# A hybrid decoder layer in one program: the attention's norm one step later, shorter GpSimd pieces, heads in another order

## The chip, the cores and the metric

The kernel runs on one core of one Trainium2 chip. The metric is the device time of one execution in microseconds (us). Five engines share the work: TensorE (PE; its weight loads are listed apart as PEld), VectorE (DVE), ScalarE (ACT), GpSimd (POOL) and SyncE (SP). SP only issues transfers here, and ACT and POOL issue some of theirs too. Each engine runs its own instructions in program order and waits for others by semaphores.

## The reference

One decoder layer, with `x` of 2048 rows by 1024 columns in float32. A mixer of three head groups is followed by a gated feed-forward network (FFN):

```python
h = _rms(x, norm_mix_g)
z = h @ w_in + b_in                    # 1024 -> 3600 columns, split among the groups
qa, ka = _rms(a_q) , _rms(a_k)         # 8 attention heads of 64 columns
ca = cumsum(log_sigmoid(a_f))          # a forgetting gate per head and row
s  = qa @ ka.T * 64**-0.5 + ca[:, None] - ca[None, :]      # causal
oa = softmax(s) @ a_v
ob = _mlstm_chunkwise(...)             # 4 heads: matrix memory in chunks of 64 rows
oc = _hgrn2_chunkwise(...)             # 4 heads: gated linear attention, chunks of 16
y  = concat(_rms(oa)*g_a, sigmoid(b_o)*_rms(ob)*g_b, silu(c_g)*_rms(oc)*g_c)
x  = x + y @ w_out
x  = x + (silu(conv3(h @ w_up).gate) * conv3(h @ w_up).up) @ w_down   # h = _rms(x), d_ff 2816
```

The attention's output is divided by its softmax sum and then normed over the 64 columns of each head (`_rms(oa)`). The attention heads don't depend on one another, so any order of them gives the same result.

## The kernel before

Matrix products keep float32 accuracy by splitting both operands into a high and a low part (`hi`, `lo`) and adding three products. The high part is a copy in a shorter format on ACT (`AF.Copy`), and the low part is the difference, mostly on POOL. Intermediate results travel through buffers in the chip's memory (`s_qh`, `s_ql`, `s_kh`, `s_kl`, `s_v`, `s_y` and others).

The program has four stages.

1. **The z stage**, up to 924 us. The columns of `z` are projected in groups of 256 (`load_split` loads a group's weights and splits them; L214 is its matmul), for each half of the rows, in the order of the table `ORDER`. Between them run the mLSTM (`phase_b`) and HGRN2 (`phase_c`) blocks, which end in `finish_heads`. Where a q or k group is done, `qk_norm_T` norms it (L418 multiplies by the inverse root on POOL), transposes it and stores it. A v group is copied into a tile per 128 rows (ACT L341, POOL L342) and stored to `s_v` (L345). In this stage each engine's order comes from the framework's scheduler, which places instructions by its own estimates.
2. **The hand-over**, 924 to 950 us, in which the last columns are finished and the first attention head is loaded (`att_load`, SP's queue, L840).
3. **The attention**, 950 to 1396 us, written in a fixed order (`manual_schedule`). A head is 40 steps: four blocks `qb` of 512 rows with 4, 8, 12 and 16 steps `j`. In a step PE computes the scores `s` (L925, L927), ACT the exponential `pf` (L931) and its high part (L933), POOL or on every fourth step DVE the low part `pl` (L937), and PE, three steps later, adds the product with V into `pv` (L950 to L952). The row maxima `mx` of a coming head (PE L874, DVE L878 and L889) run beside it. Work that is due some steps later is put into a list: `later.put(steps, f)` runs `f` that many steps on.
4. **The output projection and the FFN**, from 1396 us to the end; the change doesn't touch them.

Two users of one PSUM tile matter. `k.px` (the name x in the rows) holds in its first 260 columns the four transposes that turn a finished block (`turn`, PE L964, copied away by DVE L967), and behind them three small slots in which the norm of a whole head (`att_finish`, called when the head's last block is done, T steps in) computes its inverse root: `scale` (L1030 to L1032), then `rms_psum` (L981 to L990). `scale` is put 15 steps on. By then the next head has gone on: its block `qb` = 1 ends at the step where its `turn` is due in the same 15th step, and since `scale` was put first, it is issued first.

In the hand-over the last v group (v0) uses tiles named `h` with three buffers, which the transposed q and k (ACT L428) use as well.

Of the kernel before, what the change touches and what calls it, by code (L numbers as in the profile page):

```python
# [49 lines left out]
AHEAD = 4  # L50

ORDER = (
    "ci bv c0 c1 b0 b1 cg bo v1 v0 k0 k1 q0 q1",
    "c0 c1 ci bv b0 b1 cg bo v1 k0 q0 k1 q1 v0",
)
# [122 lines left out]
def load_split(k, wp, src, n=4):  # L178

    nc = k.nc  # L180
    width = src.shape[1]

    k.wn += 1
    at = 64 if k.wn % 2 == 0 and width == 256 else 0
    hi, lo = (
        k.t(wp, [P, 264 * DT], F32R, tag=x)[:, at : at + width * DT].rearrange("p (n c) -> p n c", c=width)
        for x in ("whi", "wlo")
    )
    for q in range(0, DT, n):
        raw = k.t(wp, [P, n, width], tag="wraw")  # L190
        nc.sync.dma_start(raw, src[q * P : (q + n) * P, :].rearrange("(dt p) c -> p dt c", p=P))
        h = hi[:, q : q + n, :]
        nc.scalar.activation(h, raw, AF.Copy)  # L193
        for i in range(0, n, 2):
            nc.gpsimd.tensor_tensor(  # L195
                lo[:, q + i : q + i + 2, :], raw[:, i : i + 2, :], h[:, i : i + 2, :].bitcast(F32), op=ALU.subtract
            )
    return hi, lo
# [64 lines left out]
def z_groups(k, hf, pz, wp, psum, xbufs, rstd=None):  # L263
# [25 lines left out]
    def nat_group(off, kind, g):  # L289
# [4 lines left out]

        store = nc.gpsimd if hf == 1 and off in (OFF_AQ + 256, OFF_AV) else nc.scalar
        bias = k.t(pz, [P, width], tag="bias")
        nc.sync.dma_start(bias, b_in[off : off + width].unsqueeze(0).broadcast_to([P, width]))
        for b in range(2):
# [3 lines left out]
            for tp in range(2):  # L302
# [32 lines left out]
                elif kind[0] == "v":  # L335
                    z4 = z.rearrange("p tt (h d) -> p tt h d", d=HD)
                    for tt in range(2):
                        v = k.t(pz, [P, 4, 130], F32R, tag="h", bufs=3)
                        nc.gpsimd.memset(v[:, :, 64:65].bitcast(F32), 1.0)
                        nc.gpsimd.memset(v[:, :, 129:130].bitcast(F32), 0.0)  # L340
                        nc.scalar.activation(v[:, :, 0:64], z4[:, tt], AF.Copy)  # L341
                        nc.gpsimd.tensor_tensor(  # L342
                            v[:, :, 65:129], z4[:, tt], v[:, :, 0:64].bitcast(F32), op=ALU.subtract
                        )
                        store.dma_start(  # L345
                            k.s_v[t0 + tt * P : t0 + (tt + 1) * P, 4 * g : 4 * g + 4, :], v.bitcast(F32)
                        )
# [60 lines left out]
def qk_norm_T(k, pz, psum, zs, ss, kind, g, store):  # L408
# [6 lines left out]
    for n, (z, hi, t0) in enumerate(zs):  # L415
        z8 = z.rearrange("p tt (h d) -> p (tt h) d", d=HD)
        r8 = rstd[:, 8 * n : 8 * n + 8].unsqueeze(2).broadcast_to([P, 8, HD])
        nc.gpsimd.tensor_tensor(z8, z8, r8, op=ALU.mult)  # L418
        ps = k.t(psum, [P, 2, 2 * P], tag="t", bufs=2)
# [242 lines left out]
def finish_heads(k, pb, num, r, gate, epsf, t0, col, sq, out):  # L662
# [12 lines left out]
    nc.vector.tensor_tensor(out, num, s.unsqueeze(2).broadcast_to([P, 16, HD]), op=ALU.mult)  # L675
    nc.gpsimd.tensor_tensor(out, out, gate.rearrange("p c (h d) -> p (c h) d", d=HD), op=ALU.mult)
    nc.gpsimd.dma_start(
# [5 lines left out]
def phase_c(k, blk, pb, psum):  # L683
# [5 lines left out]
    for j in range(2):  # L689
# [22 lines left out]
        def chunks(x):  # L712
            return x.rearrange("p (c l) -> p c l", l=P)
# [20 lines left out]
        yield  # L734
        for (r, i), eng in zip(heads, engs):
            eng.tensor_tensor(q[r, :, i, :], q[r, :, i, :], chunks(tot[r]), op=ALU.mult)
        h, lv = 1, 0
# [63 lines left out]
    for c in range(0, 4, 2):  # L801
# [4 lines left out]
        nc.vector.scalar_tensor_tensor(gc, gc, 1.0, gz, op0=ALU.add, op1=ALU.mult)  # L806
    nc.gpsimd.tensor_tensor(gate, gate, k.gbc[:, 256:512].unsqueeze(1).broadcast_to([P, 4, 256]), op=ALU.mult)
    num = oc.rearrange("p c j i d -> p (c j i) d")
# [22 lines left out]

def att_load(k, h, st):

    r = slice(h * HD, (h + 1) * HD)
    QA, KA, QB, KB = (k.t(k.pat[f"{t[1]}{h % 2}"], [P, T], F32R, tag=t) for t in ("QA", "KA", "QB", "KB"))
    V = k.t(k.pat[f"V{h % 2}"], [P, 16, 130], F32R, tag="V")
    st.update(QA=QA, KA=KA, QB=QB, KB=KB, V=V, h=h)

    def ld(dst, src):
        k.nc.sync.dma_start(dst.bitcast(F32), src)  # L840

    ld(QB[0:64], k.s_qh[r])
    ld(KB[0:64], k.s_kh[r])
    ld(QB[64:70], k.s_one[0:6])
    ld(KB[64:68], k.s_one[6:10])
    ld(KB[68:70], k.s_fc[h])
    ld(QA[0:64], k.s_qh[r])
    ld(QA[64:128], k.s_ql[r])
    ld(KA[0:64], k.s_kl[r])
    ld(KA[64:128], k.s_kh[r])  # L850
    yield
    v = k.s_v[:, h, :].rearrange("(jt p) c -> p jt c", p=P)
    ld(V[:, 0:4], v[:, 0:4])
    yield
    ld(V[:, 4:16], v[:, 4:16])

# [85 lines left out]
def att_values(k, st, pa, ps, later, qb, j, c0, ph, pl):  # L942

    nc = k.nc
    V, h = st["V"], st["h"]
    if j == 0:
# [14 lines left out]
    def turn(oT):  # L961
# [3 lines left out]
        if qb == 0:  # L965
            st["o"] = k.t(k.pat[f"o{h % 2}"], [P, 16, 65], tag="ao")
        nc.vector.tensor_copy(st["o"][:, 4 * qb : 4 * qb + 4, :], pt)  # L967

    later.put(1, out)
    if h == AH - 1:  # L970
        att_finish(k, st, pa, 4 * qb, 4, later)
    elif qb == 3:
        att_finish(k, st, pa, 0, 16, later)
# [20 lines left out]
def att_finish(k, st, pa, t0, n, later):  # L994
# [7 lines left out]
    pieces = [slice(i, i + 4) for i in range(0, n, 4)]  # L1002
    end = st["h"] == AH - 1 and t0 == 12

# [50 lines left out]
    for c in pieces:  # L1055
        later.put(i, lambda c=c: square(c))
        later.put(i + 1, lambda c=c: total(c))
        i += 1
    i = 15 if n == 16 else i + 1
    later.put(i, scale)  # L1060
# [10 lines left out]
def attention(k, pa, ps, side):  # L1071
# [4 lines left out]
    with k.tc.manual_schedule():  # L1076
        first = att_load(k, 0, sts[0])
        next(first)
        next(first)
# [821 lines left out]
```

## Time and profile before

| | |
|---|---|
| median of 3 runs | 2910.72 us (2910.49 to 2912.88) |
| profiled execution, its own time | 2909.49 us |
| its span in the trace | 2907.7 us |
| mean granted clock of PE | 0.979 |
| busy: PE / DVE / ACT / POOL | 2799.3 / 1961.4 / 1278.8 / 1446.1 us |
| share of the span | 96% / 67% / 44% / 50% |

The span is what the trace covers, from the first to the last instruction, and the execution's own time is 1.8 us longer. PE is the busiest engine by far, so time is lost only where PE waits or where its granted clock is below full speed. The chain that ended last holds only work of the FFN near the program's end; the rows of the earlier stages are therefore read from the waits of PE and from windows.

### The profile page before, as it was taken

To read this page: it belongs to the slowest core of one execution; us is meant where nothing else is said; L and a number is where in the kernel's file an instruction comes from. 1 tells how busy PE (TensorE), PEld (TensorE's weight loads), DVE (VectorE), ACT (ScalarE), POOL (GpSimd) and SP (SyncE) were. 2 spreads that over 40 slices of the span, in tenths; PEclk is the share of its full clock that TensorE was granted. 3 is DMA by queue.
4 is the path that set the end of the run, shared out by engine and by line. 5 is a ranking of instruction groups with operands and counts; after the bars stand their busy time and mean duration, and the time that the engine had idled before them with its cause. 6 is when DMAs were issued, how large, how long until landed. Compare 5 with 4: busy or idle time off the path is not lost. (4 is left out here: it accounts for less than half of the span.)

```text
span 2907.7 us, 42807 instructions
## 1 busy us (share of the span) xinstructions
PE 2799.3 (96%) x15053; PEld 2343.7 (81%) x15053; DVE 1961.4 (67%) x3523; ACT 1278.8 (44%) x2167; POOL 1446.1 (50%) x1255
## 2 busy tenths in 40 slices
PE   7999998999998999999999999999999999999999
PEld 7899996989987766666787788888788788888887
DVE  7336787265777767777446577777787577877655
ACT  4224322131322878887423344444455344344443
POOL 2345462344454668776202566666576444444543
PEclk9999997999998999999999999999999999999999
DMA  5434444333225534450456454445778333333766
GB/s 162 127 95 147 137 128 136 101 96 117 90 90 163 120 89 89 95 120 10 135 171 218 149 166 151 158 159 165 248 252 275 98 100 104 109 106 123 238 206 211
DMA packets 346616, 411.06 MB, mean 141 GB/s; under 512 B 47650, under 2 KB 234096, under 8 KB 343232
## 3 DMA queue, kind: packets, MB, share of 16 engines
q1 hardware_dynamic: 292016, 318.45, 37.0%
q10 hardware_dynamic: 51952, 81.45, 7.7%
q0 software_dynamic: 2432, 8.42, 0.8%
q8 instruction: 118, 1.93, 0.3%
q14 instruction: 98, 0.80, 0.1%
HBM read 280.24 MB, written 127.98 MB: 140 GB/s over the span
## 5 line engine op out<-in xcount | busy, mean ns | idle before, releaser
L1297 POOL TENSOR_TENSOR w<-w,w 128x512 fp32r<-128x512 f32 x302 | 404.3, 1352 | 406.0 <-ACT w L1296 334.8
L1485 PE MATMUL ps<-w,w 128*128 128x512 f32 x1848 | 422.6, 390 | 3.6 <-ACT w L1476 1.9
L1485 PEld LDWEIGHTS ps<-w,w 128*128 128x128 f32 x1848 | 347.8, 188 | 77.6 <-ACT w L1476 2.3
L214 PE MATMUL w<-whi,hlo 128*128 128x256 f32 (+1 forms) x1280 | 373.2, 292 | 0.0
L214 PE MATMUL w<-whi,hhi 128*128 128x256 f32 (+1 forms) x1280 | 370.9, 290 | 2.0 <-DVE z L330 2.0
L214 PE MATMUL w<-wlo,hhi 128*128 128x256 f32 (+1 forms) x1280 | 371.8, 291 | 0.0
L937 POOL TENSOR_TENSOR pl<-pf,ph 128x512 fp32r<-128x512 f32 (+2 forms) x240 | 287.9, 1215 | 134.1 <-ACT ph L933 89.7
L1478 POOL TENSOR_TENSOR w<-w,w 128x512 fp32r<-128x512 f32 x154 | 215.3, 1404 | 205.6 <-ACT w L1476 168.3
L1296 ACT ACTIVATE w<-w 128x512 fp32r<-128x512 f32 x302 | 180.2, 627 | 262.8 <-POOL w L1297 83.8
L1477 DVE TENSOR_TENSOR w<-w,w 128x512 fp32r<-128x512 f32 x154 | 180.0, 1177 | 104.8 <-ACT w L1475 102.9
L214 PEld LDWEIGHTS w<-whi,hhi 128*128 128x128 f32 x1280 | 247.3, 193 | 3.7 <-DVE z L330 2.4
L214 PEld LDWEIGHTS w<-wlo,hhi 128*128 128x128 f32 x1280 | 247.4, 193 | 1.6 <-issue 0.2
L214 PEld LDWEIGHTS w<-whi,hlo 128*128 128x128 f32 x1280 | 247.4, 193 | 1.3 <-issue 0.2
L195 POOL TENSOR_TENSOR wlo<-wraw,whi 128x512 fp32r<-128x512 f32 (+1 forms) x112 | 147.8, 1351 | 143.9 <-ACT whi L193 111.4
L931 ACT ACTIVATE pf<-s 128x512 f32<-128x512 f32 (+1 forms) x320 | 172.5, 539 | 81.4 <-PE s L925 40.9
L1302 DVE TENSOR_TENSOR w<-w,w 128x512 f32<-128x512 f32 x176 | 150.9, 876 | 84.3 <-DMA w<-in_w_up_dram 70.0
L933 ACT ACTIVATE ph<-pf 128x512 fp32r<-128x512 f32 (+1 forms) x320 | 185.1, 578 | 10.4
L889 DVE TENSOR_REDUCE mx<-m 128x1 f32<-128x512 f32 x192 | 130.7, 686 | 61.9 <-PE m L874 59.5
L1343 DVE SCALAR_TENSOR_TENSOR u<-ps,fcol,u 128x1023 f32<-128x1023 f32 x88 | 108.9, 1278 | 93.5 <-ACT u L1342 93.5
L1476 ACT ACTIVATE w<-w 128x512 fp32r<-128x512 f32 x154 | 96.6, 628 | 115.5 <-PE ps L1485 90.0
L874 PE MATMUL m<-KB,QB 70*128 70x512 f32 (+2 forms) x320 | 130.6, 418 | 5.6 <-DVE mx L878 5.6
L1475 ACT ACTIVATE w<-w 128x512 fp32r<-128x512 f32 x154 | 95.9, 623 | 89.4 <-POOL w L1478 46.4
(382 smaller groups left out, 7040.6 us busy)
## 6 DMA issues: line engine op xcount, KB each, us to landing
w<-in_w_up_dram SPq DMA_DIRECT2D x182, 256.0 KB
w<-s_g SPq DMA_DIRECT2D x154, 256.0 KB
w<-in_w_down_dram SPq DMA_DIRECT2D x110, 256.0 KB
wraw<-in_w_in_dram SPq DMA_DIRECT2D x48, 512.0 KB
s_g<-u ACTq DMA_DIRECT2D x88, 256.0 KB
w<-s_w SPq DMA_DIRECT2D x88, 256.0 KB
s_g<-w ACTq DMA_DIRECT2D x66, 256.0 KB
x<-in_x_dram SPq DMA_DIRECT2D x32, 512.0 KB
```

Source lines behind the costliest of these rows:

```text
L195: nc.gpsimd.tensor_tensor(lo[:, q + i : q + i + 2, :], raw[:, i : i + 2, :], h[:, i : i + 2, :].bitcast(F32), op=ALU.subtract)
L214: nc.tensor.matmul(out, lsl(lhs[a], i), rsl(rhs[b], i), start=(i == 0 and j == 0), stop=(i == n - 1 and j == 2))
L889: nc.vector.tensor_reduce(mx[:, i, kb : kb + 1], m[:, 0:n], axis=AX.X, op=ALU.max)
L931: nc.scalar.activation(pf[:, c0:], s[:, c0:], AF.Exp)
L933: nc.scalar.activation(ph[:, c0:], pf[:, c0:], AF.Copy)
L937: eng.tensor_tensor(pl[:, c0:], pf[:, c0:], ph[:, c0:].bitcast(F32), op=ALU.subtract)
L1296: nc.scalar.activation(h, t, AF.Copy)
L1297: nc.gpsimd.tensor_tensor(lo, t, h.bitcast(F32), op=ALU.subtract)
L1302: nc.vector.tensor_tensor(t, x, y, op=op)
L1477: nc.vector.tensor_tensor(gl, gr, gh.bitcast(F32), op=ALU.subtract)
L1478: nc.gpsimd.tensor_tensor(wl, wr, wh.bitcast(F32), op=ALU.subtract)
L1485: nc.tensor.matmul(tiles[tile], g[x][:, tile * P : (tile + 1) * P], w[y], start=j == 0 and c == 0, stop=j == nj - 1 and c == 2,)
```

## The change

- **The norm.** In `att_finish` the whole-head norm's `scale` is put 16 steps on instead of 15; all that follows it moves with it. It concerns the first seven heads; the last one norms its blocks one by one.
- **POOL's pieces.** Five operations on POOL are issued in pieces of a quarter to a half: the low part of the weights (L195, 512 to 256 columns), q and k times their inverse root (L418, 512 to 256), the gates in `finish_heads` (L676, 1024 to 256) and in `phase_c` (L807, 1024 to 256), and `q` times `tot` in `phase_c` (L736, 512 to 256). That makes 196 POOL instructions more.
- **The heads.** Attention runs heads 4 to 7 and then 0 to 3 (`HEADS`), and in the second half of the rows the groups k1 and q1 come before k0 and q0, so that the first head's q and k are stored a group earlier. The last q group's and v group's stores are POOL's. The last v group uses tiles `x` with two buffers instead of `h`.
- **The loads.** The first head's Q, K and V are loaded in three pieces of columns (0 to 512, 512 to 1024, 1024 to 2048), each piece with its V rows; the other heads load V in one transfer.

```diff
+HEADS = (4, 5, 6, 7, 0, 1, 2, 3)
 ORDER = (
     "ci bv c0 c1 b0 b1 cg bo v1 v0 k0 k1 q0 q1",
-    "c0 c1 ci bv b0 b1 cg bo v1 k0 q0 k1 q1 v0",
+    "c0 c1 ci bv b0 b1 cg bo v1 k1 q1 k0 q0 v0",
 )
...
-        for i in range(0, n, 2):
-            nc.gpsimd.tensor_tensor(
-                lo[:, q + i : q + i + 2, :], raw[:, i : i + 2, :], h[:, i : i + 2, :].bitcast(F32), op=ALU.subtract
-            )
+        for i in range(n):
+            nc.gpsimd.tensor_tensor(lo[:, q + i, :], raw[:, i, :], h[:, i, :].bitcast(F32), op=ALU.subtract)
...
-        store = nc.gpsimd if hf == 1 and off in (OFF_AQ + 256, OFF_AV) else nc.scalar
+        end = hf == 1 and off == OFF_AV
+        store = nc.gpsimd if hf == 1 and off in (OFF_AQ, OFF_AV) else nc.scalar
...
-                        v = k.t(pz, [P, 4, 130], F32R, tag="h", bufs=3)
+                        v = k.t(pz, [P, 4, 130], F32R, **({"tag": "x", "bufs": 2} if end else {"tag": "h", "bufs": 3}))
...
-        nc.gpsimd.tensor_tensor(z8, z8, r8, op=ALU.mult)
+        for i in range(0, 8, 4):
+            zi = z8[:, i : i + 4, :]
+            nc.gpsimd.tensor_tensor(zi, zi, r8[:, i : i + 4, :], op=ALU.mult)
...
-    nc.gpsimd.tensor_tensor(out, out, gate.rearrange("p c (h d) -> p (c h) d", d=HD), op=ALU.mult)
+    for c in range(4):
+        oc = out[:, 4 * c : 4 * c + 4, :]
+        nc.gpsimd.tensor_tensor(oc, oc, gate[:, c, :].rearrange("p (h d) -> p h d", d=HD), op=ALU.mult)
...
-        for (r, i), eng in zip(heads, engs):
-            eng.tensor_tensor(q[r, :, i, :], q[r, :, i, :], chunks(tot[r]), op=ALU.mult)
+        for r, i in heads:
+            for c in range(0, 4, 2):
+                qi = q[r, c : c + 2, i, :]
+                nc.gpsimd.tensor_tensor(qi, qi, chunks(tot[r])[:, c : c + 2, :], op=ALU.mult)
...
-    nc.gpsimd.tensor_tensor(gate, gate, k.gbc[:, 256:512].unsqueeze(1).broadcast_to([P, 4, 256]), op=ALU.mult)
+    for c in range(4):
+        nc.gpsimd.tensor_tensor(gate[:, c, :], gate[:, c, :], k.gbc[:, 256:512], op=ALU.mult)
...
-    ld(QA[0:64], k.s_qh[r])
-    ld(QA[64:128], k.s_ql[r])
-    ld(KA[0:64], k.s_kl[r])
-    ld(KA[64:128], k.s_kh[r])
-    yield
     v = k.s_v[:, h, :].rearrange("(jt p) c -> p jt c", p=P)
-    ld(V[:, 0:4], v[:, 0:4])
-    yield
-    ld(V[:, 4:16], v[:, 4:16])
+    parts = ((0, 4), (4, 8), (8, 16)) if n == 0 else ((0, 16),)
+    for j0, j1 in parts:
+        c = slice(j0 * P, j1 * P)
+        ld(QA[0:64, c], k.s_qh[r, c])
+        ld(QA[64:128, c], k.s_ql[r, c])
+        ld(KA[0:64, c], k.s_kl[r, c])
+        ld(KA[64:128, c], k.s_kh[r, c])
+        ld(V[:, j0:j1], v[:, j0:j1])
+        yield
...
-    i = 15 if n == 16 else i + 1
+    i = 16 if n == 16 else i + 1
     later.put(i, scale)
...
         first = att_load(k, 0, sts[0])
         next(first)
-        next(first)
```

The first place is on DVE in the attention, while the second head runs and the first head is normed. Before, from the last maximum ahead of the norm (names ending in numbers are buffers; `ao` is the head's output, `ass` the sums of squares, `x` the shared PSUM tile):

```order
L895 TENSOR_REDUCE m_1744_10847<-mx_10558 128x4
L1030 RECIPROCAL x_9750<-ao_10012 128x16
L1031 TENSOR_TENSOR ass_1682_10656<-ass_1682_10656,x_9750 128x16
L1032 TENSOR_TENSOR x_9750<-ass_1682_10656,x_9750 128x16
L981 TENSOR_SCALAR x_9750<-x_9750 128x16
L982 TENSOR_SCALAR a16h_10855<-x_9750 128x16
L983 TENSOR_SCALAR x_9750<-x_9750 128x16
L967 COPY ao_10721<-x_9750 128x260
L866 MEMSET mx_10874 128x16
```

And now (line numbers of the changed kernel are 12 higher in these functions):

```order
L907 TENSOR_REDUCE m_1744_11050<-mx_10762 128x4
L979 COPY ao_10924<-x_9946 128x260
L878 MEMSET mx_11069 128x16
L890 ISA m_11071,mx_11069<-m_11071,mnat 128x128
L890 ISA mx_11069 128x1
L1042 RECIPROCAL x_9946<-ao_10216 128x16
L1043 TENSOR_TENSOR ass_1682_10859<-ass_1682_10859,x_9946 128x16
L1044 TENSOR_TENSOR x_9946<-ass_1682_10859,x_9946 128x16
L993 TENSOR_SCALAR x_9946<-x_9946 128x16
L994 TENSOR_SCALAR a16h_11080<-x_9946 128x16
L995 TENSOR_SCALAR x_9946<-x_9946 128x16
```

The six small operations of the norm stood ahead of the copy that takes the next head's turned block out of `x`; now they stand behind it, and behind the first maximum of the step after.

The second place is on ACT, the end of the z stage and the first exponential of the attention. Before (`h` from `z` are the v copies, `h` from `t` the transposed q and k):

```order
L341 ACTIVATE h_9584<-z_9533 128x4x64
L341 ACTIVATE h_9590<-z_9533 128x4x64
L428 ACTIVATE h_9438<-t_9512,col 128x512
L428 ACTIVATE h_9492<-t_9523,col 128x512
L341 ACTIVATE h_9647<-z_9596 128x4x64
L341 ACTIVATE h_9653<-z_9596 128x4x64
L931 ACTIVATE pf_9803<-s_9799 128x512
```

And now:

```order
L344 ACTIVATE x_9780<-z_9729 128x4x64
L344 ACTIVATE x_9786<-z_9729 128x4x64
L433 ACTIVATE h_9632<-t_9707,col 128x512
L344 ACTIVATE x_9843<-z_9792 128x4x64
L433 ACTIVATE h_9686<-t_9719,col 128x512
L344 ACTIVATE x_9849<-z_9792 128x4x64
L943 ACTIVATE pf_10008<-s_10004 128x512
```

The v copies go to `x` instead of `h`, and the third of them stands between the two transposed tiles rather than behind both.

The third place is on POOL, at the same time. Before (`b_qk` is the mLSTM's last gate, `z` by `rstd` the last q group):

```order
L342 TENSOR_TENSOR h_9584<-z_9533,h_9584 128x4x64
L345 DMA s_v<-h_9584 128x520
L676 TENSOR_TENSOR b_qk_7318<-b_qk_7318 128x1024
L418 TENSOR_TENSOR z_9386<-z_9386,rstd_9495 128x512
L418 TENSOR_TENSOR z_9441<-z_9441,rstd_9495 128x512
L339 MEMSET h_9590 128x4
L340 MEMSET h_9590 128x4
L342 TENSOR_TENSOR h_9590<-z_9533,h_9590 128x4x64
L677 DMA s_y<-b_qk_7318 128x4x256
```

And now:

```order
L345 TENSOR_TENSOR x_9786<-z_9729,x_9786 128x4x64
L348 DMA s_v<-x_9780 128x520
L423 TENSOR_TENSOR z_9580<-z_9580,rstd_9689 128x256 x2
L423 TENSOR_TENSOR z_9635<-z_9635,rstd_9689 128x256 x2
L348 DMA s_v<-x_9786 128x520
L342 MEMSET x_9843 128x4
L343 MEMSET x_9843 128x4
L683 TENSOR_TENSOR b_qk_7465<-b_qk_7465 128x256 x4
L436 DMA s_qh<-h_9632 128x2x256
L345 TENSOR_TENSOR x_9843<-z_9792,x_9843 128x4x64
```

The multiplication of q by its inverse root stands ahead of the mLSTM's gate now, each in pieces; behind the gate come the stores of q, among them the v tile's.

## Rows read from the trace of the kernel before

**Rows 1.** Windows by stage: us; busy (instructions) PE PEld DVE ACT POOL; clock, DMA share, GB/s.

```profile
0.00:924.00 924.00, 875.75 (x6237) 812.86 (x6237) 582.07 (x1300) 277.54 (x445) 381.52 (x418) 0.97 0.38 120
924.00:950.00 26.00, 18.03 (x56) 12.08 (x57) 16.35 (x44) 7.48 (x15) 13.80 (x24) 0.61 0.79 213
950.00:1396.00 446.00, 423.42 (x2153) 298.07 (x2152) 330.57 (x832) 367.68 (x697) 322.63 (x278) 0.98 0.40 86
```

**Rows 2.** Waits of PE, 950 to 1396: waiting <- releaser: sum us, count, longest.

```profile
PE x L964 <- DVE x L983: 13.9, 7, 3.4
PE pv L952 <- DVE pl L937: 5.2, 10, 1.0
PE pv L952 <- POOL pl L937: 3.3, 5, 1.3
```

**Rows 3.** Timeline of PE around the first head's norm: start, duration, instruction, wait.

```profile
1020.98 0.40 PE L952 MATMUL pv<-pl,V 128*65 128x512 f32 x1
...
1023.04 0.44 PE L964 MATMUL x<-ident,oT 65*128 65x65 f32 x4 [1.67 <-DVE x L983]
```

**Rows 4.** Timeline of DVE at the same place.

```profile
1021.58 0.25 DVE L1030 RECIPROCAL x<-ao 128x16 f32<-128x16 f32 x1
...
1022.71 0.18 DVE L983 TENSOR_SCALAR x<-x 128x16 int32<-128x16 int32 x1
```

**Rows 5.** Windows of low clock, in the attention (three) and the z stage (two).

```profile
1024.30:1027.70 3.40, 3.40 (x10) 2.39 (x9) 1.47 (x10) 2.25 (x4) 1.27 (x1) 0.50 0.02 5
1082.30:1089.10 6.80, 6.80 (x21) 4.80 (x22) 2.06 (x12) 2.76 (x5) 1.64 (x2) 0.50 0.00 0
...
1369.00:1375.80 6.80, 5.37 (x16) 3.61 (x16) 4.30 (x25) 2.76 (x5) 2.27 (x3) 0.50 0.09 19
437.00:512.00 75.00, 60.61 (x274) 48.91 (x274) 53.85 (x125) 20.88 (x35) 19.08 (x20) 0.77 0.42 133
780.00:847.00 67.00, 58.41 (x426) 56.04 (x425) 59.72 (x113) 16.59 (x25) 39.52 (x35) 0.90 0.35 106
```

**Rows 6.** Timeline of DVE and POOL, 815 to 823.

```profile
817.25 1.25 DVE L131 TENSOR_TENSOR hu<-hu,hh 128x16 f32<-128x16 f32 x1
822.30 0.18 DVE L132 SCALAR_TENSOR_TENSOR rstd<-hu,rstd 128x16 f32<-128x16 f32 x1
...
817.00 5.23 POOL L195 TENSOR_TENSOR wlo<-wraw,whi 128x512 fp32r<-128x512 f32 x4
```

**Rows 7.** Groups of POOL by shape, 0 to 924: count | busy, mean ns | idle before.

```profile
L195 POOL TENSOR_TENSOR wlo<-wraw,whi 128x512 fp32r<-128x512 f32 x96 | 126.8, 1352 | 127.9 <-ACT whi L193 98.2 <-issue 17.4 <-DMA wraw<-in_w_in_dram 10.9
L418 POOL TENSOR_TENSOR z<-z,rstd 128x512 f32<-128x512 f32 x30 | 36.5, 1236 | 45.2 <-DVE rstd L132 36.7 <-issue 3.8 <-DVE f_s L674 3.2
L342 POOL TENSOR_TENSOR h<-z,h 128x256 fp32r<-128x256 f32 x29 | 24.0, 834 | 28.2 <-ACT h L341 27.9
```

**Rows 8.** Waits of PE in the z stage, 0 to 924, four of them.

```profile
PE b L573 <- DVE cstate L790: 4.4, 1, 4.4
PE t L172 <- DVE hlo L175: 3.9, 3, 3.2
PE b L621 <- DVE att L727: 3.7, 1, 3.7
PE b L748 <- DVE c L766: 3.6, 2, 2.8
```

**Rows 9.** Timeline of PE, ACT and POOL in the hand-over.

```profile
933.30 1.48 PE L874 MATMUL m<-KB,QB 70*128 70x512 f32 x3 [5.47 <-DVE mx L878]
...
930.28 0.42 ACT L341 ACTIVATE h<-z 128x256 fp32r<-128x256 f32 x1 [10.36 <-DMA s_v<-h]
940.35 0.60 ACT L931 ACTIVATE pf<-s 128x512 f32<-128x512 f32 x1 [3.32 <-PE s L927]
...
921.75 0.57 POOL L345 DMA_DIRECT2D s_v<-h  x1 [0.30 <-POOL h L342]
...
930.25 0.10 POOL L339 MEMSET h<- 128x4 f32 x1 [3.54 <-DMA s_v<-h]
```

More of the change, by code (lines that the diff above doesn't have):

```diff
@@ L829, in drain, with att_load @@
             self.step()
-def att_load(k, h, st):
+def att_load(k, n, st):
+    h = HEADS[n]
     r = slice(h * HD, (h + 1) * HD)
-    QA, KA, QB, KB = (k.t(k.pat[f"{t[1]}{h % 2}"], [P, T], F32R, tag=t) for t in ("QA", "KA", "QB", "KB"))
-    V = k.t(k.pat[f"V{h % 2}"], [P, 16, 130], F32R, tag="V")
-    st.update(QA=QA, KA=KA, QB=QB, KB=KB, V=V, h=h)
+    QA, KA, QB, KB = (k.t(k.pat[f"{t[1]}{n % 2}"], [P, T], F32R, tag=t) for t in ("QA", "KA", "QB", "KB"))
+    V = k.t(k.pat[f"V{n % 2}"], [P, 16, 130], F32R, tag="V")
+    st.update(QA=QA, KA=KA, QB=QB, KB=KB, V=V, h=h, n=n)
     def ld(dst, src):
@@ L944, in att_values @@
     nc = k.nc
-    V, h = st["V"], st["h"]
+    V, n = st["V"], st["n"]
     if j == 0:
@@ L965, in turn @@
         if qb == 0:
-            st["o"] = k.t(k.pat[f"o{h % 2}"], [P, 16, 65], tag="ao")
+            st["o"] = k.t(k.pat[f"o{n % 2}"], [P, 16, 65], tag="ao")
         nc.vector.tensor_copy(st["o"][:, 4 * qb : 4 * qb + 4, :], pt)
     later.put(1, out)
-    if h == AH - 1:
+    if n == AH - 1:
         att_finish(k, st, pa, 4 * qb, 4, later)
@@ L1002, in att_finish @@
     pieces = [slice(i, i + 4) for i in range(0, n, 4)]
-    end = st["h"] == AH - 1 and t0 == 12
+    end = st["n"] == AH - 1 and t0 == 12
     def first():
```

## The prediction

> **What bounds the kernel now.** I read the windows by stage first, then the waits of PE in each stage, then the timelines around the longest of these waits, and last the windows of low clock. In the attention PE is busy for 423.4 of 446.0 us [rows 1]; DVE, ACT and POOL have between 78 and 123 us to spare there. The 22.6 us in which PE is idle are almost all in three kinds of wait: 13.9 us in seven waits of the transposes (L964) for the norm on DVE (L983), 5.2 and 3.3 us in fifteen short waits for the low part of the exponentials [rows 2]. So PE sets the attention's pace, and what PE doesn't wait there is gained one for one, until the next engine is late. The z stage has PE busy for 875.8 of 924 us [rows 1]: 48 us of idle time, spread over many small waits, and 381.5 us of POOL work in 924. The hand-over of 26 us has PE busy for 18.0, at a mean clock of 0.61 [rows 1]. The output projection and the FFN, from 1396 us to the end, have the same instructions before and after; I cost them at nothing.
>
> **The norm one step later.** The first seven heads have it. In the first, PE's last product of the block began at 1020.98, and its transposes only at 1023.04 after a wait of 1.67 us [rows 3]. In that gap DVE does the six norm operations, from 1021.58 to 1022.71 + 0.18 = 1022.89 [rows 4]. Both write the tile `x`, and `scale` is issued ahead of `turn`. In the new order the copy of the turned block stands before the norm, so the transposes wait for nothing of the norm. All seven waits have this cause, so 13.9 us go.
>
> What is late next? DVE then does the norm's 1.3 us one step later, in front of a maximum (L890) instead of the copy. The maxima belong to a later head and have a lead of many steps; the norm's result is needed only by its own products, which move with it. The low part that DVE makes on every fourth step is the one thing close behind: today's worst wait for it is 1.0 us [rows 2]. That is the rival below. I take the whole 13.9.
>
> There is a second part. PE's granted clock was 0.50 of full speed, 1.2 instead of 2.4 GHz, in four short stretches of the attention: from 1024.3 to 1027.7, from 1082.3 to 1089.1, once more for 3.4 us, and from 1369.0 to 1375.8 [rows 5]. The first begins 1.3 us after the transposes that waited, and the others likewise follow such a wait within about 3 us. Work at half clock takes double the time, so half of PE's busy time in them is lost: 1.7 + 3.4 + 1.7 + 2.7 = 9.5 us. Three of the seven waits were followed by no drop, so a wait alone doesn't make one, and I take 6 of the 9.5. The sum for the norm: 13.9 + 6 = 20 us gained. The bounds: 25 when all 23.4 and some of the short waits go, 7 when each place gives back 1.0 us and the clock nothing.
>
> **The short pieces on POOL.** They add 196 instructions, 112 of them in the low part of the weights. A piece of 512 columns takes 1352 ns, one of 256 columns 834 [rows 7], though of other lines. Two short ones take 1668, so a piece more costs 0.316 us, and 196 of them 62 us of POOL. In the z stage POOL is idle for 924 - 381.5 = 542 us [rows 1], mostly waiting for ACT's high parts [rows 7]; that idle time hides the 62 us unless they fall in a chain that PE waits for. The pieces of L418 do lie in such a chain, between the norm of q or k and PE's transposes: 30 more pieces by 0.316 make 9.5 us if none is hidden. That is the upper end, 10 us lost.
>
> The Trainium skill ("GPSIMD Engine Reference", section 3.1) speaks against pieces too: two software dispatch hops per instruction. Its 4497 ns for 2048 elements at 2.6 cycles each and 1.2 GHz would leave about 60 ns for them, an estimate; 196 pieces would then be 12 us of POOL, and the 30 of L418 2 us. By that the pieces would lose 2 us at most, and the sum would stay.
>
> What the pieces can win is time of DVE. At 817.25 a DVE operation on 16 columns took 1.25 us while POOL had four pieces of L195 back to back; at 822.30, between pieces, one of that size took 0.18 [rows 6]. DVE's small operation ended with POOL's piece. With pieces of 0.83 us, such an operation waits at most some 0.8. In chains of many small operations (the inverse roots, the chunk states) this shortens the chain by up to a third, and PE waits for the ends of such chains: four groups of such waits sum to 4.4 + 3.9 + 3.7 + 3.6 = 15.6 us [rows 8]. A third of it is 5 us. The clock fell behind these waits too, to a mean of 0.77 from 437 to 512 us and 0.90 from 780 to 847 [rows 5], which costs (1 - 0.77) x 75 + (1 - 0.90) x 67 = 24 us; a fifth of it is another 5. I take 10 us gained. The lower bound is all 15.6 and a third of the clock, 24 gained; the upper is the 10 lost.
>
> DVE's order in the z stage changes everywhere, as the scheduler reacts to other durations. That is the largest unknown, and nothing in the profile bounds it but what the present order costs: a bad stretch is worth up to 32 us (the third rival).
>
> **Heads, stores and loads.** In the hand-over PE waits 5.47 us for a maximum until 933.30 [rows 9]. DVE's maximum stands behind the transposed q's low part, that behind ACT's transposed tile, and that behind the v copy, which waited 10.36 us for a buffer `h` whose store of 921.75 landed only at 930.2 (the memset at 930.25 waited for the same) [rows 9]. With `x` for these tiles the transposed tiles no longer queue behind that landing, and POOL does q's multiplication ahead of the gate: I expect the maxima some 5 us earlier. But the first exponential, at 940.35 [rows 9], gains less. In the new order its tile has to wait for the landing of a v store, which POOL issues only after the gate's four pieces, the stores of q and the v copy, and which runs beside the pieces of Q, K and V and head 5's loads. A landing under load took 930.2 - 922.3 = 7.9 us [rows 9]. Counted from the stage's start at 924 [rows 1], the first exponential came 16.4 us later; I expect 13 to 20. The second and third pieces of Q and K stand in SP's queue behind V's first piece, which waits for PE's last projection to free its memory. I take nothing for the whole part, between 6 gained and 8 lost (about one landing).
>
> **The sum.** From the profiled execution of 2909.5 us: -20 (norm), -10 (pieces), 0 (hand-over) make 2879.5. The median of the runs is 1.2 above the profiled execution, so 2881 us.
>
> **The rivals.**
>
> *The wait is given back.* After the transposes, PE waits for DVE's low part at each of the seven places, at today's longest 1.0 us, and the clock drops stay, since a gap remains. For it: DVE's norm still takes 1.3 us beside a busy PE. Against it: of 10 such waits the mean is 0.5, with DVE busy for 74% of the stage. The norm then brings 6.9, and the time is 2909.5 - 6.9 - 10 + 1.2 = 2894. Chance 0.11; with nothing from the pieces either it would be 2904, at the edge.
>
> *The pieces bring nothing.* DVE's total work and its order decide the z stage's waits, and its operations wait as long in sum behind more, shorter pieces. For it: the pieces that run back to back keep POOL as busy as before, and four pieces take longer than one long. Then 2909.5 - 20 + 1.2 = 2891. Chance 0.16.
>
> *A new bad stretch in the z stage: slower.* The scheduler's new DVE order puts one more stretch like that of 437 to 512 us. It costs 75 - 60.6 = 14.4 us of idle PE. At a mean clock of 0.77 another 0.23 x 75 = 17.2 us go [rows 5]. Together 31.6, with the pieces' 10 gone: 2909.5 - 20 + 31.6 + 1.2 = 2922. It decides from about 26 us lost, where it eats the norm's 20 and goes beyond 0.2%. For it: this stretch came out of the scheduler in the kernel before, so one can come again. Against it: PE's own order changes only between some 50 and 340 us, and POOL's work is the same. Chance 0.08.
>
> *Everything comes.* Norm 23.4 with all of the clock, pieces 20, the hand-over 3 gained: 2909.5 - 46.4 + 1.2 = 2864. Chance 0.10.
>
> The forecast itself has 0.55, and its own range is 2868 to 2893.
>
> **How the numbers follow.** This kernel's runs differ by 0.1%, and I call 0.2%, 5.8 us, what a measurement can tell from no change: 2904.9 to 2916.5 is the same. Slower holds three quarters of the third rival, 0.06. The same holds its remaining 0.02, the part of the first where the pieces bring nothing, 0.03, and 0.01 of the second, together 0.06. Faster is the rest, 0.88. The range of 2862 to 2903 leaves out the 0.12 of same and slower and some 0.05 of the last rival's far end.
>
> **What would show it.** The norm is right if the waits of the transposes for the norm are gone from PE's list, and if the attention's window has PE idle for under 10 us with fewer stretches at 0.50. The pieces are right if small DVE operations beside L195 take about 0.8 instead of 1.25 us and the four waits of rows 8 shrink. The hand-over is right if PE's 5.5 us wait for a maximum shrinks and ACT's first exponential waits for a landing, 13 to 20 us after the z stage's end. I am wrong if the z stage ends later than 924 us, or if PE's waits for the low part grow by as much as the norm's go.

## The result and the profile after

The changed kernel takes 2882.13 us (median of 4 runs, 2879.12 to 2883.02), the kernel before 2911.8 us beside it. The ratio is 0.990, with a 95% interval of 0.9885 to 0.9914: 29 us faster, between 25 and 33. The prediction was 2881, in a range of 2862 to 2903. The profiled execution has a span of 2877.0 us, 30.7 less than before.

To see where they are, both spans are cut at the same marks of the program: the end of PE's last projection, PE's first and its last product with V. First the changed kernel (columns as in [rows 1]):

```profile
0.00:913.10 913.10, 871.64 (x6239) 810.02 (x6240) 559.95 (x1298) 277.14 (x446) 418.99 (x616) 0.97 0.38 121
913.10:934.40 21.30, 13.68 (x44) 8.71 (x43) 14.88 (x41) 5.63 (x12) 12.11 (x21) 0.60 0.99 286
934.40:1378.00 443.60, 433.34 (x2230) 307.45 (x2228) 336.60 (x845) 374.31 (x712) 330.10 (x285) 0.99 0.40 87
1378.00:2877.00 1499.00, 1470.08 (x6545) 1210.86 (x6544) 1027.29 (x1340) 620.36 (x998) 720.30 (x531) 0.99 0.52 171
```

And the kernel before at these marks:

```profile
0.00:923.80 923.80, 875.73 (x6237) 812.86 (x6237) 582.07 (x1300) 277.54 (x445) 381.32 (x418) 0.97 0.38 120
923.80:945.70 21.90, 13.75 (x44) 8.96 (x44) 13.54 (x38) 6.11 (x13) 13.51 (x23) 0.61 0.74 213
945.70:1408.90 463.20, 440.57 (x2230) 310.69 (x2228) 336.06 (x846) 375.32 (x713) 329.43 (x284) 0.97 0.39 85
1408.90:2907.70 1498.80, 1469.27 (x6544) 1211.22 (x6544) 1029.74 (x1340) 619.88 (x998) 721.85 (x531) 0.99 0.52 171
```

The z stage is 10.7 us shorter, the hand-over 0.6, the attention 19.6, and the rest is the same to 0.2. The prediction had 10, 0 and 20. That the rest agrees so closely is partly chance: in the fourteen profiles of this case it takes between 1494.1 and 1506.7 us, though no edit touches it. In the attention PE's idle time goes from 463.20 - 440.57 = 22.6 to 443.60 - 433.34 = 10.3 us, which is 12.4 less; the other 7.2 us are PE's own busy time, which is shorter for the same instructions.

PE's waits in the attention, where [rows 2] had 13.9 us for the norm:

```profile
PE pv L964 <- DVE pl L949: 8.3, 9, 2.0
PE pv L964 <- POOL pl L949: 1.7, 1, 1.7
...
PE x L976 <- ACT oT L970: 0.7, 1, 0.7
```

The waits for the norm are gone, and those for DVE's low part have grown from 5.2 to 8.3 us. At the place of [rows 3] and [rows 4], PE and DVE now run like this:

```profile
1009.55 0.39 PE L964 MATMUL pv<-pl,V 128*65 128x512 f32 x1
1009.78 0.41 PE L976 MATMUL x<-ident,oT 65*128 65x65 f32 x4
```

```profile
1010.22 0.43 DVE L979 COPY ao<-x 128x260 f32<-128x260 f32 x1
...
1011.09 0.26 DVE L1042 RECIPROCAL x<-ao 128x16 f32<-128x16 f32 x1
```

PE goes from the product to the transposes without a gap, and DVE begins the norm after the copy.

The low clock, where [rows 5] had four stretches of 20.4 us in the attention and two bad ones in the z stage:

```profile
435.90:456.40 20.50, 16.17 (x66) 12.99 (x65) 15.93 (x43) 5.21 (x10) 4.00 (x7) 0.50 0.39 125
463.20:483.70 20.50, 16.04 (x61) 13.19 (x61) 16.93 (x52) 5.06 (x7) 6.57 (x14) 0.50 0.36 125
...
1347.30:1350.70 3.40, 3.40 (x10) 2.40 (x9) 3.06 (x14) 2.03 (x4) 0.83 (x2) 0.50 0.00 0
1357.50:1360.90 3.40, 3.40 (x13) 2.31 (x12) 0.85 (x3) 1.53 (x3) 3.28 (x4) 0.50 0.60 136
```

In the attention two stretches of 3.4 us are left. They follow the two longest waits for the low part, near the end of the attention:

```profile
1346.39 0.45 PE L964 MATMUL pv<-pl,V 128*65 128x512 f32 x1 [1.96 <-DVE pl L949]
...
1357.16 0.45 PE L964 MATMUL pv<-pl,V 128*65 128x512 f32 x1 [1.67 <-POOL pl L949]
```

In the z stage the one from 780 to 850 is gone, but the one around 440 to 480 has stayed and got worse, from a mean clock of 0.81 to 0.75 between 430 and 520 us, before and after:

```profile
430.00:520.00 90.00, 75.40 (x370) 61.94 (x369) 61.12 (x141) 25.59 (x45) 21.26 (x21) 0.81 0.40 126
```

```profile
430.00:520.00 90.00, 74.07 (x347) 60.74 (x346) 60.95 (x146) 25.86 (x45) 23.04 (x39) 0.75 0.38 126
```

This is the window from 780 to 908 before and after:

```profile
780.00:908.00 128.00, 119.42 (x916) 113.59 (x914) 106.01 (x232) 33.69 (x57) 65.72 (x69) 0.95 0.31 100
```

```profile
780.00:908.00 128.00, 123.99 (x1002) 118.49 (x1001) 101.97 (x248) 35.48 (x60) 72.60 (x104) 1.00 0.36 114
```

PE is idle for 4.0 instead of 8.6 us in it, and the clock no longer falls, (1 - 0.95) x 128 = 6.4 us: 11 us, about the stage's whole gain. Of the four waits of [rows 8], the first and the third have nearly gone, the second is as before, and the fourth (L748 for DVE's c) has no row any more; the waits for q or k from POOL have grown from 1.9 to 3.8 us:

```profile
PE t L174 <- DVE hlo L177: 3.9, 2, 3.6
PE t L427 <- POOL z L423: 3.8, 6, 1.0
...
PE b L626 <- DVE att L734: 1.0, 1, 1.0
...
PE b L578 <- DVE cstate L799: 0.4, 1, 0.4
```

And the hand-over, against [rows 9], on PE, ACT and POOL:

```profile
917.56 1.48 PE L886 MATMUL m<-KB,QB 70*128 70x512 f32 x3 [3.21 <-DVE mx L890]
```

```profile
930.41 0.60 ACT L943 ACTIVATE pf<-s 128x512 f32<-128x512 f32 x1 [13.18 <-DMA s_v<-x]
```

```profile
922.75 1.10 POOL L348 DMA_DIRECT2D s_v<-x  x2
```

The first maxima come 913.1 + 4.5 instead of 923.8 + 9.5, 5 us earlier as forecast, and the first exponential waits for a v store, 17.3 us after the last projection (16.5 before).

### The profile page after: what moved, and what is told of

The parts are those of the page before. It is cut to its first block, busy times and chain, and to the rows that moved or that the text cites. A ratio compares the mean times of both kernels' runs of the same rounds, so it can differ in the third digit from the quotient of the medians.

```text
span 2877.0 us, 42992 instructions
## 1 busy us (share of the span) xinstructions
PE 2788.7 (97%) x15053; PEld 2337.0 (81%) x15053; DVE 1938.7 (67%) x3523; ACT 1277.4 (44%) x2167; POOL 1481.5 (51%) x1451
## 5 line engine op out<-in xcount | busy, mean ns | idle before, releaser
L198 POOL TENSOR_TENSOR wlo<-wraw,whi 128x256 fp32r<-128x256 f32 (+1 forms) x224 | 171.7, 804 | 107.0 <-ACT whi L195 79.8
L945 ACT ACTIVATE ph<-pf 128x512 fp32r<-128x512 f32 (+1 forms) x320 | 185.1, 579 | 10.2
```

Of the source, the lines that this page charges most:

```text
L198: nc.gpsimd.tensor_tensor(lo[:, q + i, :], raw[:, i, :], h[:, i, :].bitcast(F32), op=ALU.subtract)
L945: nc.scalar.activation(ph[:, c0:], pf[:, c0:], AF.Copy)
```

## The experiments

Each kernel's ratio is to runs of the kernel before on the same chip. In microseconds, 0.001 is 2.9. Where two changed kernels are compared, the interval given is an estimate from the two intervals of their ratios.

**The parts, one at a time.** First the norm alone, and the changed kernel with the norm put back.

```diff
-    i = 15 if n == 16 else i + 1
+    i = 16 if n == 16 else i + 1
```

> The kernel before with the norm's scale 16 instead of 15 steps on, nothing else. Theory (the norm's waits and the clock that fell behind them): 18 to 20 us faster than before, about 2892, the attention's window shorter by that, z stage and hand-over unchanged. Rival (the waits go, the clock's stretches come and go by other causes): 12 to 14 us faster, about 2898. Rival (given back by waits for the low part): under 8 us faster.

Measured 2891.74 us, ratio 0.9923 (0.9902 to 0.9943): 22 us faster, between 17 and 29. The theory's 18 to 20 lie within, those of both rivals outside. Its attention lasts 441.9 us instead of 463.2. The z stage, with instructions in the same order as before, took 928.5 us here and 923.8 in the first profile, so one stage of one profile can be 5 us off.

> The changed kernel with the norm's scale back at 15 steps. Theory: 18 to 20 us slower than the changed kernel, about 2901, with the seven waits of the transposes for the norm back (about 14 us). Rival (by the heads' new order the wait doesn't matter): within 3 us of the changed kernel.

Measured 2898.43 us, ratio 0.9947 (0.9930 to 0.9964), 14 us slower than the changed kernel by the two ratios (some 7 to 20), and 20.6 by the attention in the profiles (464.2 against 443.6), at the edge of that interval. The profiled execution of this kernel was one of its slower ones (2903.41 us), that of the changed kernel its fastest (2879.12). The attention and PE's wait:

```profile
939.60:1403.80 464.20, 441.73 (x2230) 311.28 (x2228) 335.90 (x846) 375.30 (x712) 329.79 (x285) 0.97 0.39 82
```

```profile
PE x L976 <- DVE x L995: 13.9, 7, 3.4
```

The seven waits are back to the tenth of a microsecond. In this kernel six of the seven come with a stretch at half clock that begins within 1.5 us of the wait's end (the last one 0.6 us ahead of it); the first and the last of these stretches:

```profile
1016.40:1019.80 3.40, 3.40 (x12) 2.52 (x11) 1.19 (x7) 1.23 (x2) 0.86 (x2) 0.50 0.02 5
1364.50:1371.30 6.80, 6.16 (x18) 3.99 (x19) 3.70 (x21) 2.79 (x6) 1.48 (x2) 0.50 0.09 20
```

So the clock's part belongs to these waits: it returns with them, at the same places. The rival in which the clock comes and goes by itself falls. The other profiles say the same. In the eight kernels with `scale` at 15 steps the attention takes 461.2 to 466.5 us, and 43 of their 56 waits come with a stretch that begins within 2 us of the wait's end. In the six with 16 it takes 441.9 to 443.6 us, and in none of them does such a stretch begin in the attention before its last 31 us.

Then the pieces alone (the diff's five POOL edits on the kernel before), and the heads, order, tiles and loads alone (the change without pieces and norm).

> The kernel before with the five kinds of short pieces on POOL, nothing else. Theory (short pieces shorten what DVE waits for): about 11 us faster, 2900, all of it in the z stage. Rival (the z stage's 10.8 us come from the new order of the q and k groups, or the order that the scheduler makes of it): within 3 us of before.

Measured 2904.32 us, ratio 0.9967 (0.9955 to 0.9980): 10 us faster, as the theory had it; the z stage ends at 917.5.

> The changed kernel without the short pieces and with the norm at 15 steps: heads 4 to 7 first, the order of the groups, the tiles x, the loads in pieces. Theory: within 3 us of before (2909 to 2914). Rival (the z stage's gain is of the new order): about 11 us faster, 2900.

Measured 2912.8 us, ratio 0.9990 (0.9979 to 1.0001): no change that can be told, so the theory holds. Its z stage ends at 926.6. The three parts alone sum to 22 + 10 + 3 = 35 us, against 29 measured together (25 to 33); the interval of the norm alone is wide enough for the difference.

**Which pieces.** Here my reason was tested: the low parts' pieces alone, and the other four kinds alone.

```diff
-        for i in range(0, n, 2):
-            nc.gpsimd.tensor_tensor(
-                lo[:, q + i : q + i + 2, :], raw[:, i : i + 2, :], h[:, i : i + 2, :].bitcast(F32), op=ALU.subtract
-            )
+        for i in range(n):
+            nc.gpsimd.tensor_tensor(lo[:, q + i, :], raw[:, i, :], h[:, i, :].bitcast(F32), op=ALU.subtract)
```

> The kernel before with only the weights' low parts (L195) in pieces of 256 columns. Theory (each kind of piece acts through the waits of DVE behind it; the wait of 2.76 us near 837 and the low clock around it come from L195's chain): 5 to 8 us faster, about 2904 beside a before of 2911, the low clock between 830 and 847 gone. Rival (the gates' 2.4 us pieces do all of it): within 2 us of before.

Measured 2915.54 us, ratio 1.0007 (0.9994 to 1.0019): nothing that can be told, and the theory's 5 to 8 us lie outside. Yet DVE's small operations did become shorter, before and now:

```profile
L131 DVE TENSOR_TENSOR hu<-hu,hh 128x16 f32<-128x16 f32 x48 | 18.5, 386 | 1.0
```

```profile
L131 DVE TENSOR_TENSOR hu<-hu,hh 128x16 f32<-128x16 f32 x48 | 10.1, 210 | 1.0
```

In the z stage DVE is busy for 561.2 instead of 582.1 us, and the stage ends at 928.6. PE now waits for other things, first of all for q or k from POOL, 8.6 us where it had been 1.9:

```profile
PE t L420 <- POOL z L416: 8.6, 5, 5.2
```

> The kernel before with only the other four kinds of short pieces (z by rstd, the two gates, q by tot). Theory: 3 to 5 us faster, the wait of 3.67 us near 787 and the low clock behind it gone, the one near 837 still there. Rival (the gates do all of it): 9 to 11 us faster. Rival (the added pieces of the q and k norm cost as much as the rest brings): within 2 us of before.

Measured 2902.86 us, ratio 0.9963 (0.9951 to 0.9975): 11 us faster (7 to 14), all that the five kinds bring by the timed runs. My theory of both kinds sharing it falls. The size is the first rival's, 9 to 11; whether the gates do it alone is tested next.

The gates alone, and q by tot alone:

```diff
-    nc.gpsimd.tensor_tensor(out, out, gate.rearrange("p c (h d) -> p (c h) d", d=HD), op=ALU.mult)
+    for c in range(4):
+        oc = out[:, 4 * c : 4 * c + 4, :]
+        nc.gpsimd.tensor_tensor(oc, oc, gate[:, c, :].rearrange("p (h d) -> p h d", d=HD), op=ALU.mult)
...
-    nc.gpsimd.tensor_tensor(gate, gate, k.gbc[:, 256:512].unsqueeze(1).broadcast_to([P, 4, 256]), op=ALU.mult)
+    for c in range(4):
+        nc.gpsimd.tensor_tensor(gate[:, c, :], gate[:, c, :], k.gbc[:, 256:512], op=ALU.mult)
```

> The kernel before with only the two gates (L676 and L807) in four pieces each, nothing else. After the two runs before this, the theory is that only POOL's longest instructions count, the 2.4 us behind which DVE's chains stood near 787: 8 to 11 us faster, the window from 780 to 908 with the clock at 0.99 or above and PE idle for under 5 us instead of 8.6. Rival (the other pieces, or the order that the scheduler makes, bring it): within 3 us of before.

Measured 2909.05 us, ratio 0.9979 (0.9969 to 0.9988): 6 us faster (3 to 9), with the z stage ending at 921.4. From 780 to 908 the clock is at 1.00, as forecast, but PE is still idle for 8.7 us, where the theory had under 5. The time lies between theory and rival, and the gates don't do it alone.

```diff
-        for (r, i), eng in zip(heads, engs):
-            eng.tensor_tensor(q[r, :, i, :], q[r, :, i, :], chunks(tot[r]), op=ALU.mult)
+        for r, i in heads:
+            for c in range(0, 4, 2):
+                qi = q[r, c : c + 2, i, :]
+                nc.gpsimd.tensor_tensor(qi, qi, chunks(tot[r])[:, c : c + 2, :], op=ALU.mult)
```

> The kernel before with only q by tot (L736) in two pieces, nothing else. Theory: within 3 us of before, with PE idle for 8 us or more from 780 to 908. Rival (the HGRN2 chain on POOL and DVE is shortened, or the scheduler's new order brings it): 5 to 11 us faster.

Measured 2901.81 us, ratio 0.9953 (0.9941 to 0.9965): 14 us faster (10 to 17), against my theory. Its z stage ends at 924.4, within what the kernels without it show. What its trace has is a short hand-over, 16.2 us instead of 21.9:

```profile
924.40:940.60 16.20, 13.32 (x44) 8.29 (x42) 13.66 (x39) 5.88 (x13) 9.73 (x20) 0.66 0.67 222
```

There the scheduler put the last stores in another order on POOL: the last v store begins 10.4 instead of 14.5 us after the last projection, and the first exponential 10.2 instead of 16.5. The z stage gains 3 to 8 us late, as the next paragraphs show; ahead of that this profile had fallen 5 us behind, as that of the norm alone did with unchanged instructions. The attention is 1.8 and the rest 4.8 us shorter, though the edit touches neither; how far that comes from the edit is open.

The ends of the z stage hide part of this, since the profiles differ by up to 5 us before the pieces act. They can be compared from a later mark. Every kernel has the same 4640 matmuls of the projections, so the last 990 of them are the same work; in the kernel before they begin at 740 us.

| kernel | begin at (us) | last 990 projections (us) |
|---|---|---|
| before; norm alone; heads alone | 740.0; 745.0; 743.3 | 183.8; 183.5; 183.3 |
| low parts' pieces alone | 745.8 | 182.8 |
| gates alone | 741.6 | 179.8 |
| q by tot alone | 745.2 | 179.3 |
| four kinds without the low parts (rest_only; v_act_no_split below) | 741.7; 739.6 | 176.5; 176.3 |
| all five kinds, in six kernels | 739.6 to 744.1 | 173.4 to 173.5 |

So the pieces gain their 10 us here, and every kernel with all five gains them. With marks between 680 and 785 us the partial kernels move by some 2 us, as the other work between the projections changes places: the gates bring 1 to 4 us, q by tot 3 to 8, the four kinds 6 to 9, the low parts alone -2 to 1. Beside the four kinds, though, the low parts bring about another 3 us, too little for the timed runs to tell. Each edit also gives the scheduler other orders to choose, and no run kept the order fixed; whether the shorter pieces act by themselves or by the order is not shown.

**The hand-over.** Three variants of the changed kernel: the last v tiles among the three buffers `h`, as before; the first head's loads in one piece; and the last v stores issued by ACT.

```diff
-    v = k.t(pz, [P, 4, 130], F32R, **({"tag": "x", "bufs": 2} if end else {"tag": "h", "bufs": 3}))
+    v = k.t(pz, [P, 4, 130], F32R, tag="h", bufs=3)
```

> The changed kernel with the last v group's tiles back among the three buffers h. Theory (x frees the maxima, but the first exponential then waits for a v store's landing, so little is gained): within 2 us of the changed kernel, the wait for the first maxima back at 5 us or more. Rival (the tiles x are what keeps the hand-over from getting longer): 4 to 8 us slower than the changed kernel.

Measured 2890.26 us, ratio 0.9916 (0.9899 to 0.9934), 5 us slower than the changed kernel by the two ratios, which the interval (-2 to 11) doesn't tell from none. The profile speaks for the rival: the hand-over takes 29.8 us instead of 21.3, and at most 22.5 us in the twelve profiles that have both the tiles `x` and the loads in pieces, or neither. ACT waits for buffers again and for the last v stores' landing, and PE for ACT:

```profile
927.29 0.42 ACT L344 ACTIVATE h<-z 128x256 fp32r<-128x256 f32 x1 [8.76 <-DMA s_v<-h]
...
942.45 0.63 ACT L945 ACTIVATE ph<-pf 128x512 fp32r<-128x512 f32 x1 [12.85 <-DMA s_v<-h]
```

```profile
943.50 0.58 PE L936 MATMUL s<-QB,KB 70*128 70x256 f32 x1 [11.97 <-ACT pf L943]
```

The wait for the first maxima stayed at 3.2, so what I had named as the tiles' use is not what they do here: they bring the v stores forward. The last one begins 14.9 us after the last projection without them, and 10.2 with them.

```diff
-    parts = ((0, 4), (4, 8), (8, 16)) if n == 0 else ((0, 16),)
+    parts = ((0, 16),)
```

> The changed kernel with the first head's loads in one piece each, like the other heads'. Theory (the first exponential waits for a v store's landing, not for the loads): within 2 us of the changed kernel, ratio to before 0.989 to 0.992. Rival (the pieces let the first maxima and scores begin early): 4 to 8 us slower than the changed kernel, the first scores on PE later by as much, counted from the last projection.

Measured 2894.59 us, ratio 0.9931 (0.9919 to 0.9943), 9 us slower than the changed kernel by the two ratios (some 4 to 15); the hand-over takes 35.3 us. The rival is right on the size, within the interval, and on the start: an early v store lands later, so ACT waits for its buffer, the maxima follow, and PE's first scores come 15.0 instead of 10.3 us after the last projection:

```profile
922.07 0.42 ACT L344 ACTIVATE x<-z 128x256 fp32r<-128x256 f32 x1 [5.56 <-DMA s_v<-x]
```

```profile
924.44 1.48 PE L886 MATMUL m<-KB,QB 70*128 70x512 f32 x3 [7.80 <-DVE mx L890]
```

The theory is right on the wait of the first exponential, which has become longer:

```profile
929.91 1.10 POOL L348 DMA_DIRECT2D s_v<-x  x2
```

```profile
946.78 0.60 ACT L943 ACTIVATE pf<-s 128x512 f32<-128x512 f32 x1 [22.05 <-DMA s_v<-x]
```

From the issue of these two stores to the exponential that waits for them it is 946.78 - 929.91 = 16.9 us. With the loads in pieces it is 930.41 - 922.75 = 7.7. That is 9.2 of the 14 us; the rest lies ahead of the issue. The median v store between 905 and 950 us took 6.2 us from issue to landing with the pieces and 13.3 without:

```profile
s_v<-x POOLq DMA_DIRECT2D x4, 260.0 KB, 6.2
```

```profile
s_v<-x POOLq DMA_DIRECT2D x4, 260.0 KB, 13.3
```

In both kernels the transfer engines are busy for nearly the whole hand-over (a share of 0.99 and 0.98), and the edit changes nothing but how the first head's loads are cut and ordered, so that decides here when the store lands.

```diff
-        store = nc.gpsimd if hf == 1 and off in (OFF_AQ, OFF_AV) else nc.scalar
+        store = nc.gpsimd if hf == 1 and off == OFF_AQ else nc.scalar
```

> The changed kernel with the last v group's stores issued by ACT instead of POOL. Theory (the first exponential waits 5.8 us for a landing because POOL issues the store behind the stores of q): the first exponential 3 to 5 us earlier counted from the last projection, the time 3 to 5 us under the changed kernel. Rival (the landing is late because the transfers are loaded, whoever issues): within 1 us of the changed kernel. Rival (ACT's first exponentials are held up by its own issuing): 1 to 3 us slower.

Measured 2883.62 us, ratio 0.9889 (0.9870 to 0.9908), not to be told from the changed kernel. The stores are issued some 4 us earlier, but the wait has moved from the store to a load:

```profile
931.37 0.77 PE L937 MATMUL s<-QA,KA 128*128 128x512 f32 x1 [4.29 <-DMA KA<-s_kh]
```

The first exponential comes 16.5 us after the last projection instead of 17.3, not the 3 to 5 us earlier of my theory. Last, the same kernel with the low parts in one piece:

> The changed kernel with the last v group's stores on ACT, and with the weights' low parts in one piece of 512 columns again. Theory (the low parts' pieces bring nothing): within 3 us of the kernel with them and the stores on ACT, whose ratio to before was 0.989. Rival (beside the other pieces they do shorten DVE's chains): 4 to 8 us slower, ratio 0.991 or above.

Measured 2886.34 us, ratio 0.9899 (0.9883 to 0.9914), with the z stage ending at 915.9 where the kernel with pieces has 915.8. By the two ratios the low parts' pieces bring 3 us (-4 to 10), which is no more than the timed runs could tell apart. No version beat the changed kernel by more than the interval.

## Why the prediction was right

*The norm.* Right in mechanism and size. The seven waits are gone, 13.9 us; 3.1 are given back at DVE's low part and 1.6 gained at POOL's, which makes 12.4 of idle time. I had taken the whole 13.9, and PE idle for under 10 us; it is 10.3. The rival that a wait is given back holds for a fifth: six waits of 0.92 to 0.97 us for the low part stand where ones of 0.30 to 0.83 stood. The clock's part was taken as 6: by the stretches at half clock it is 9.5 - 3.4 = 6.1, and PE's busy time is 7.2 shorter; what the other 1.1 is stays open. That the clock's part belongs to the waits was argued from four places, and the kernel with the norm put back shows it at six.

*The pieces.* The sum was right (10 forecast; 10.7 in the profile, 10 alone), and of the two bad stretches named, the one from 780 to 847 went. The other, which I had costed higher, stayed. The 10 was made of two chosen fractions, a third of 15.6 and a fifth of 24, so that it came out to a microsecond is luck. The reason was half wrong. I reasoned from the low parts' pieces, behind which DVE's small operations waited [rows 6]. Those operations did get shorter, from 386 to 210 ns in the kernel with these pieces alone, and the time did not move: the step that failed is "this shortens the chain ... and PE waits for the ends of such chains". What brings most of the time are the other kinds, the 2.4 us gates among them with 6 us alone; the low parts add about 3 us beside them late in the stage. The price of a piece, 0.316 us, was too high on the mean. The changed kernel's POOL groups are, against [rows 7]:

```profile
L198 POOL TENSOR_TENSOR wlo<-wraw,whi 128x256 fp32r<-128x256 f32 x192 | 148.2, 809 | 88.6 <-ACT whi L195 61.4 <-DMA wraw<-in_w_in_dram 11.0 <-DMA s_kl<-l 8.5
...
L423 POOL TENSOR_TENSOR z<-z,rstd 128x256 f32<-128x256 f32 x64 | 41.9, 685 | 57.7 <-DVE rstd L134 43.7 <-ACT b_qk L670 10.1 <-issue 3.6
```

Two pieces cost 2 x 809 - 1352 = 266 ns more than one in L198, and 2 x 685 - 1236 = 134 in L423. For q by tot (L745) it is 313, as priced, and each added piece of the gate in `phase_c` (L817), whose operand is read in another form too, costs 427. All of POOL's stage grew by 419.0 - 381.3 = 37.7 us instead of 62, that is 192 ns for an added piece on the mean, and its idle time hid it. The Trainium skill's figures ("GPSIMD Engine Reference", section 3.1) had given an estimate of 60 ns per piece; the rows show more, 134 to 427, and they decide.

*The hand-over.* Zero was right, and so was the wait that would take over: the first exponential waits for a v store's landing, 17.3 us after the last projection (forecast 13 to 20). But the zero is a balance of larger sizes than I gave, 6 gained to 8 lost: in the profiles it is 14 us longer without the pieces of the loads and 8.5 without the tiles `x`. The earlier maxima I had put down to these tiles and to POOL's order; without the tiles they come as early.

*The slower rival.* The z stage got no new bad stretch, but the one near 440 to 480 got worse, by 0.06 x 90 = 5 us of clock, and the mark at 740 us comes at 739.6, no earlier to speak of. So such trades happen: with the low parts' pieces alone the wait of 3.7 us near 787 shrank to 1.2, and one of 5.2 for q or k came. Two arguments against the rival were wrong. POOL works 37.7 us more, and PE's order changes behind 340 us too: products of the HGRN2 block (`b` from `q` and `c`) at 548 us, for instance, now stand some 200 matmuls of the projections earlier.

## What to carry to other kernels

A wait on an engine that is never the bound can be the cheapest thing to remove: look for two users of one tile, and for the order in which they are issued in the same step. A shorter instruction on a helping engine is worth something only where the bounding engine waits for what stands behind it, so follow the chain to that wait before counting it. Where a tile's next use waits for a store, look at the loads that are under way beside it: cutting them was worth 9 us here, while issuing the store some 4 us earlier only moved the wait to a load. And before reading a few microseconds from two profiles, look at how far a stage that nobody touched differs between them.

## What the runs showed of the hardware that was not expected

- Waits of PE of 1.67 to 3.42 us for the norm came with 3.4 us or more at half clock in 43 of 56 places in the eight kernels that have them. In the changed kernel six waits of about 0.95 us for the low part, one per head, were followed by none, and those of 1.96 and 1.67 us by 3.4 us each.
- Two stores of 260 KB each took 7.7 or 16.9 us from their issue to the instruction that waited for them, in the same place of the program, by how the loads beside them are cut.
- The z stage with the same instructions took 923.8 and 928.5 us in two profiles, and the untouched rest of the program 1494.1 to 1506.7 in fourteen, so a single profile tells changes below some 5 us from nothing only with the timed runs beside it. From 740 us to its end, though, the z stage took 173.4 to 173.5 us in all six kernels with the same pieces, so a part of a stage can repeat far better than the whole.
